# Second layer norm in another group order, and the last quarter of the output norm on ScalarE and GpSimd, in a decoder layer on one Trainium2 core

## The chip, the cores and the metric

The kernel runs on one core of a Trainium2 chip. The metric is device time in microseconds. The core's engines run their own instruction streams in order and wait for one another through semaphores: TensorE (PE, matrix multiply, transposes), VectorE (DVE), ScalarE (ACT), GpSimd (POOL) and SyncE (SP, which here only issues DMAs).

## The reference

One layer of a decoder trunk on 256 tokens of width 2048, in float32. Each of three sub-layers adds its output to the scaled residual and normalises:

```python
h = x
h = layer_norm(ALPHA * h + hybrid_mixer(h, ...), ln_g[0], ln_b[0])
h = layer_norm(ALPHA * h + memory_cross_attention(h, mem, ...), ln_g[1], ln_b[1])
h = layer_norm(ALPHA * h + conv_ffn(h, ...), ln_g[2], ln_b[2])      # the output

def layer_norm(x, g, b):
    mu = mean(x); var = mean((x - mu)**2)
    return (x - mu) * rsqrt(var + 1e-5) * g + b

def conv_ffn(h, w_up, conv_w, conv_b, w_down):
    u = causal_depthwise_conv3(h @ w_up) + conv_b     # 2 x 5632 columns
    a, g = split(u, 2)
    return (a * gelu(g)) @ w_down
```

## The kernel before, in words

Every large matrix product is done as three float32r products: both operands are split into a high part (a cast on ScalarE, L296) and a low part (a subtraction on VectorE, L297), and TensorE computes high x high, high x low and low x high (`mm3` at L311 to L313 with the weights stationary, `mm3x` at L319 to L321 with the activations stationary). Weights come in chunks of 128 x 1024 (512 KB) through SP's queue. There are four buffers of raw chunks, and three each of high and low parts.

The program is written in the order of the model and a scheduler sets the order on each engine, by priorities ("lanes": `first` before `split` before `mixer` before `proj`) and by a simulated time line. Where the code wants a certain order on one engine it adds one by hand with `after(ins, other)`, which makes `ins` come after `other` without a semaphore. That order is fixed at build time.

The residual `R` holds 2 x 128 tokens ("token 0" and "token 1" below are the two halves of 128 tokens) by 2048 columns.

**Output projections.** `to_residual` goes through five column groups (512, 512, 512, 256, 256 columns). The products of a group are added to `R` (L423) and its batch-norm statistics taken (L427). The last `late` groups are done for token 0 first and then for token 1, so that work on token 0 can lie beside token 1's matmuls: after token 0's last group, and after each group of token 1, `next(beside)` emits one more piece of that work. In the cross-attention's projection `late` is 4, so this loop holds the groups at columns 512, 1024, 1536 and 1792, of 24, 24, 12 and 12 matmuls for each token; in the FFN's down projection it is 1.

**Layer norm.** `statistics` aggregates the statistics of a token half (L1125), adds epsilon (L1126), and gets 1/sqrt from ScalarE as exp(-0.5 ln v) (L1127, L1128), with one Newton step in four small VectorE instructions (L1129 to L1132). `normalise` needs two VectorE instructions for each column group: subtract the mean and multiply by the gain (L1149), then multiply by 1/sqrt and add the bias (L1154). `layer_norm_of` then transposes 128-column tiles on TensorE (L1163), and `split_on_pe` makes the two parts in PSUM: cast on ScalarE (L1171), subtraction on TensorE by a product with a negated identity (L1172), cast again (L1174). These features are the right-hand side of the FFN's up projection, whose first three tiles (`to_rows_of`) go through features of columns 0 to 1023 first and 1024 to 2047 after.

In the second layer norm token 0 has four groups of 512 columns and token 1 has six (128, 128, 256, 512, 512, 512). With `NORM0 = 3` three groups of token 0 are emitted beside token 1's projection, and `NORM1 = (2,)` emits the fourth after token 1's third. `holds` puts the low part of the FFN's second and third weight chunk behind two of the normalise instructions, which `HOLD` picks from the list of them.

**The end.** `last_norm(0)` lies beside token 1's last column group, `last_norm(1)` follows it: four groups of 512 columns, each stored with a DMA, in turn from ScalarE's and SP's queue.

Of the kernel before, what the change touches and what calls it, by code (L numbers as in the profile page):

```python
# [8 lines left out]
F32 = mybir.dt.float32  # L9
# [6 lines left out]
D = 2048  # L16
# [19 lines left out]
CST_AT = 3  # L36
SKEW = 16
MOVING_AT = {512: 48, 256: 32}
NORM0, NORM1, HOLD = 3, (2,), 2
TABLE_PACE, SCAN_PACE = 0.8, 2.8  # L40
BUCKET_FROM = [16, 21, 27, 35, 46, 59, 77, 99, 128, 166, 216]

# [156 lines left out]
class Program:  # L199
    def __init__(self, tc, a, out, ctx):  # L200
        self.tc, self.nc, self.a, self.out, self.ctx = tc, tc.nc, a, out, ctx
        pool = lambda name, bufs, **kw: ctx.enter_context(tc.tile_pool(name=name, bufs=bufs, **kw))
        self.lanes = {"first": 0, "split": 100_000, "mixer": 200_000, "proj": 300_000,
                      "late": 400_000}
        self.cur_lane, self.turns = "mixer", False
        self.holds = []
        self.background, self.pace, self.credit = None, 0.0, 0.0
        self.last_hi = self.last_lo = self.last_mm = None
        self.mm_marks = [None, None, None]
        self.bv = Behind(self, self.nc.vector, lambda: self.last_lo)  # L210
        self.bs = Behind(self, self.nc.scalar, lambda: self.last_hi)
        self.bt = Behind(self, self.nc.tensor, lambda: self.mm_marks[-2])
        tc.cur_priority = self.lanes["mixer"]
        self.consts = pool("consts", 1)
        self.wraw = pool("wraw", 4)
        self.whi = pool("whi", 3)
        self.wlo = pool("wlo", 3)
        self.gap("a", 192)
        self.acts = pool("acts", 1)
        self.stat = pool("stat", 2)  # L220
        self.pj = pool("pj", 3, space=bass.MemoryType.PSUM)
        self.op = pool("op", 1, space=bass.MemoryType.PSUM)
        self.mx = pool("mx", 2, space=bass.MemoryType.PSUM)
        self.pq = pool("pq", 1, space=bass.MemoryType.PSUM)
        self.dram = pool("dram", 1, space=bass.MemoryType.DRAM)
# [89 lines left out]
    def mm3x(self, ps, hi, lo, ah, al, start, stop):  # L315

        mm = self.nc.tensor.matmul
        with self.lane("proj"):
            mm(ps, ah, hi, start=start, stop=False)  # L319
            mm(ps, ah, lo, start=False, stop=False)  # L320
            self.last_mm = mm(ps, al, hi, start=False, stop=stop)  # L321

# [37 lines left out]
    def to_residual(self, w, X, k0, k1, scaled=True, final=True, load=None, late=0, keep=(),  # L360
# [31 lines left out]
        for tok in range(2):  # L392
            left = [(k1 - k0) * n // 1024 for _, n in RES_COLS[early:]]
            ps = {}
            for i in order:
                g, c0, n, ks, src = chunks[i]
                if i not in held:
                    held[i] = self.weights(src, into=keep[i] if i in fixed else None, cols=n)
                new = g not in ps
                if new:  # L400
                    ps[g] = self.pj.tile([128, 512], F32, name="pj")
                left[g] -= 1
                self.chunk_cols(ps[g], held[i], X, tok, n, ks, new, left[g] == 0)
                if left[g] == 0:
                    self.add(ps[g][:, :n], tok, c0, n, scaled, final)
                    if beside is not None:
                        next(beside, None)
            if tok == 0:
                beside = between()
                next(beside, None)  # L410
                again = order[len(keep):-turning]
# [706 lines left out]
    def statistics(self, toks):  # L1118

        V, S, n = self.nc.vector, self.nc.scalar, len(toks)  # L1120
        with self.lane("first"):
            mv = self.stat.tile([128, 2, 2], F32, name="mv")
            v, y, t = (self.stat.tile([128, 2], F32, name=i)[:, :n] for i in ("vv", "yy", "ty"))
            for i, tok in enumerate(toks):
                V.bn_aggr(mv[:, i, :], self.st[:, tok])  # L1125
            V.tensor_scalar(v, mv[:, :n, 1], EPS, None, ALU.add)  # L1126
            S.activation(y, v, ACTF.Ln)  # L1127
            S.activation(y, y, ACTF.Exp, scale=-0.5)  # L1128
            V.tensor_mul(t, y, y)  # L1129
            V.tensor_mul(t, t, v)  # L1130
            V.tensor_scalar(t, t, -0.5, 1.5, ALU.mult, ALU.add)
            V.tensor_mul(y, y, t)  # L1132
        return [(mv[:, i, 0:1], y[:, i:i + 1]) for i in range(n)]

    def load_gb(self, i):
# [23 lines left out]
    def transposes(self, pairs):  # L1159

        last = None
        for dst, src in pairs:
            ins = self.nc.tensor.matmul(dst, src, self.ident, is_transpose=True,  # L1163
                                        start=last is None, stop=True, skip_group_check=True)
            if last is not None:
                self.after(ins, last)
            last = ins

    def split_on_pe(self, ps, h):

# [25 lines left out]
    def layer_norm_of(self, tok, H, edges):  # L1196
# [3 lines left out]
        for c0, c1 in self.normalise((tok,), norm, edges):  # L1200
            kk = min(4, (c1 - c0) // 128)
            for k in range(c0 // 128, c1 // 128, kk):
                ps = self.mx.tile([128, kk, 128], F32, name="mx")
                self.transposes([(ps[:, j, :], self.R[:, tok, (k + j) * 128:(k + j + 1) * 128])
                                 for j in range(kk)])
                self.split_features(ps, H, k, kk, slice(tok * 128, tok * 128 + 128))
            yield

# [70 lines left out]
    def ffn(self, H):  # L1279
# [2 lines left out]
        p = self.ctx.enter_context(self.tc.tile_pool(name="ffp", bufs=1))  # L1282
        w = self.ctx.enter_context(self.tc.tile_pool(name="ffw", bufs=2))
        cv = p.tile([128, NFF, 2, 4], F32, name="cv")
        nc.scalar.dma_start(cv, a["conv"].rearrange("p (i j c) -> p i j c", i=NFF, j=2))
        act = [self.acts.tile([128, KD, 2, 256], F32R, name="A", tag="A"),
               p.tile([128, NFF - KD, 2, 256], F32R, name="act")]
        act = Parts(*[t[:, i:i + 4] for t in act for i in range(0, t.shape[1], 4)])
# [24 lines left out]
            pass  # L1313

    def last_norm(self, tok):
        norm = self.statistics((tok,))
        for i, (c0, c1) in enumerate(self.normalise((tok,), norm, range(0, D + 1, 512))):
            (self.nc.sync if i % 2 else self.nc.scalar).dma_start(
                self.out[tok * 128:tok * 128 + 128, c0:c1], self.R[:, tok, c0:c1])
            yield  # L1320


# [19 lines left out]
```

## Time and profile before

| | |
|---|---|
| median of 3 runs | 1284.87 us (1282.33 to 1287.47) |
| the profiled execution | 1284.53 us |
| its span in the profile | 1282.4 us |
| TensorE busy | 1250.7 us (98%) |
| VectorE busy | 882.1 us (69%) |
| ScalarE busy | 659.7 us (51%) |
| GpSimd busy | 18.9 us (1%) |

The span is the time between the first and the last instruction or transfer that the profiler saw; start-up and completion lie around it. Times in rows count from the span's start. A row of the order of instructions has start, duration, engine, line, operation, output<-inputs, shape and count; in square brackets is the idle time of the engine before it and what ended it. A row of the table of stretches has the stretch, its length, then busy time and number of instructions of PE, PEld (weight load), DVE, ACT and POOL, the granted TensorE clock as a share of full speed, the DMA engines' share and GB/s. A busy TensorE is not a fast one: the number of matmuls in a stretch and the granted clock tell that.

### The profile page before, as it was taken

How to read it: one execution, taken by the hardware profiler on the slowest of the kernel's cores; microseconds unless marked ns; L12 is line 12 of the kernel's file. 1: busy time of each engine (PE TensorE's matmuls, PEld its weight loads, DVE VectorE, ACT ScalarE, POOL GpSimd, SP SyncE). 2: the span in 40 equal slices, each digit the busy share in tenths (PEclk: the TensorE clock that was granted, in tenths of full speed). 3: DMA queues.
4: the chain of work that ended last, by engine and by line, in shares of the span. 5: the costliest groups of instructions: out<-in, count | busy, mean ns of one | idle time of the engine just before them, and what ended most of it. 6: DMA issues, size and time to landing. Idle time of an engine off the chain costs nothing.

```text
span 1282.4 us, 23034 instructions
## 1 busy us (share of the span) xinstructions
PE 1250.7 (98%) x9222; PEld 1157.6 (90%) x9222; DVE 882.1 (69%) x1507; ACT 659.7 (51%) x1032; POOL 18.9 (1%) x34
## 2 busy tenths in 40 slices
PE   7999999899999999899999999999999999999996
PEld 7788889898789899699999999999999988888896
DVE  7899898777675666866666666666666654554557
ACT  6884436566563356355555555555555543334342
POOL 0200001000000000000000000000000000000000
PEclk9999999999999999999999999999999999999998
DMA  8663347743356554355555555655565755656573
GB/s 291 196 179 117 116 133 209 217 133 132 122 191 246 188 207 149 121 165 194 191 192 197 194 189 194 198 193 188 195 198 192 255 194 197 192 185 198 186 240 131
DMA packets 67350, 237.37 MB, mean 185 GB/s; under 512 B 7787, under 2 KB 8604, under 8 KB 66476
## 3 DMA queue, kind: packets, MB, share of 16 engines
q1 hardware_dynamic: 64720, 230.21, 54.4%
q0 software_dynamic: 1424, 4.33, 1.7%
q8 instruction: 72, 1.18, 0.4%
q10 hardware_dynamic: 1100, 1.38, 0.3%
q14 instruction: 34, 0.28, 0.1%
HBM read 231.82 MB, written 2.49 MB: 183 GB/s over the span
## 4 chain that ended last, share of the span: by engine, by line
PE 89%; DMA 4%; DVE 3%; ACT 3%; issue 1%; POOL 0%; SPq 0%; ACTq 0%; DVEq 0%
PE pj L311 17%; PE pj L313 17%; PE pj L312 17%; PE pj L319 10%; PE pj L320 10%; PE pj L321 10%; DMA raw<-in_win_u 2%; PE pa L1053 2%; DMA s5us<-Ec 1%; DMA raw<-in_win_c 1%; ACT hi L296 1%; PE pa L191 1%; DVE lo L297 1%; PE mx L882 1%; PE mx L1016 1%
## 5 line engine op out<-in xcount | busy, mean ns | idle before, releaser
L297 DVE TENSOR_TENSOR lo<-raw,hi 128x1024 fp32r<-128x1024 f32 (+2 forms) x403 | 488.5, 1212 | 338.1 <-ACT hi L296 336.6
L296 ACT CAST hi<-raw 128x1024 fp32r<-128x1024 f32 (+2 forms) x403 | 419.6, 1041 | 510.4 <-PE pj L312 279.1
L312 PE MATMUL pj<-mix,hi 128*128 128x256 f32 x1380 | 382.2, 277 | 0.0
L311 PE MATMUL pj<-mix,hi 128*128 128x256 f32 x1380 | 381.7, 277 | 0.0
L313 PE MATMUL pj<-mix,lo 128*128 128x256 f32 x1380 | 381.4, 277 | 0.0
L311 PEld LDWEIGHTS pj<-mix,hi 128*128 128x128 f32 x1380 | 259.6, 188 | 0.2
L312 PEld LDWEIGHTS pj<-mix,hi 128*128 128x128 f32 x1380 | 259.4, 188 | 0.1
L313 PEld LDWEIGHTS pj<-mix,lo 128*128 128x128 f32 x1380 | 259.4, 188 | 0.0
L311 PE MATMUL pj<-A,hi 128*128 128x256 f32 x496 | 140.7, 286 | 6.7 <-ACT hi L296 6.6
L313 PE MATMUL pj<-A,lo 128*128 128x256 f32 x496 | 138.7, 287 | 3.6 <-DVE lo L297 3.5
L312 PE MATMUL pj<-A,hi 128*128 128x256 f32 x496 | 139.2, 284 | 0.0
L311 PEld LDWEIGHTS pj<-A,hi 128*128 128x128 f32 x496 | 94.7, 192 | 9.5 <-ACT hi L296 7.5
L313 PEld LDWEIGHTS pj<-A,lo 128*128 128x128 f32 x496 | 93.4, 192 | 7.9 <-DVE lo L297 5.1
L320 PE MATMUL pj<-lo,act 128*128 128x512 f32 (+1 forms) x280 | 96.3, 345 | 0.0
L321 PE MATMUL pj<-hi,act 128*128 128x512 f32 (+1 forms) x280 | 96.3, 345 | 0.0
L312 PEld LDWEIGHTS pj<-A,hi 128*128 128x128 f32 x496 | 94.6, 192 | 1.6 <-issue 1.6
L320 PE MATMUL pj<-lo,A 128*128 128x512 f32 (+2 forms) x288 | 95.9, 334 | 0.0
L321 PE MATMUL pj<-hi,A 128*128 128x512 f32 (+2 forms) x288 | 95.4, 332 | 0.0
L319 PE MATMUL pj<-hi,A 128*128 128x512 f32 (+2 forms) x288 | 90.7, 333 | 0.0
L319 PE MATMUL pj<-hi,act 128*128 128x512 f32 (+1 forms) x280 | 89.3, 345 | 0.0
L320 PEld LDWEIGHTS pj<-lo,A 128*128 128x128 f32 x288 | 54.1, 188 | 6.5 <-issue 1.1
L321 PEld LDWEIGHTS pj<-hi,A 128*128 128x128 f32 x288 | 54.2, 188 | 5.0
(325 smaller groups left out, 1809.6 us busy)
## 6 DMA issues: line engine op xcount, KB each, us to landing
raw<-in_w_up SPq DMA_DIRECT2D x176, 512.0 KB, 3.4
raw<-in_w_down SPq DMA_DIRECT2D x92, 512.0 KB, 4.3
raw<-in_win_c SPq DMA_DIRECT2D x48, 512.0 KB, 4.3
raw<-in_w_out SPq DMA_DIRECT2D x32, 512.0 KB, 3.4
raw<-in_win_sv SPq DMA_DIRECT2D x8, 512.0 KB, 4.9
raw<-in_wk_m SPq DMA_DIRECT2D x8, 512.0 KB, 4.3
raw<-in_wv_m SPq DMA_DIRECT2D x8, 512.0 KB, 4.0
raw<-in_wq SPq DMA_DIRECT2D x8, 512.0 KB, 4.4
```

What stands on the lines that cost most here:

```text
L191: ins = getattr(self.engine, name)(*args, **kw)
L296: self.last_hi = nc.scalar.copy(hi[:, :n], raw[:, :n])
L297: self.last_lo = nc.vector.tensor_sub(lo[:, :n], raw[:, :n], hi[:, :n].bitcast(F32))
L311: mm(ps, hi, ah, start=start, stop=False)
L312: mm(ps, hi, al, start=False, stop=False)
L313: self.last_mm = mm(ps, lo, ah, start=False, stop=stop)
L319: mm(ps, ah, hi, start=start, stop=False)
L320: mm(ps, ah, lo, start=False, stop=False)
L321: self.last_mm = mm(ps, al, hi, start=False, stop=stop)
L882: mm(h_ps[:, 0:75].rearrange("p (g n) -> p g n", g=5), w1[:, i * 128:i * 128 + 128], kv[:, :, 2 * l:2 * l + 16 * NC_ - 15:16], start=l == ...
L1016: mm(zs, q[:, t, gl, qs], kh[:, 0:m], start=True, stop=False)
L1053: ins = mm(o[64 * r:64 * r + 64, gl, 128 * c:256], vv[:, c, v, :], pt[:, k0:k1], start=start[r] is None, stop=False, skip_group_check=True)
```

## The change

Five parts:

- The second layer norm emits two groups of token 0 beside token 1's projection in place of three (`NORM0`), and the other two after token 1's fourth and fifth group (`NORM1`). `HOLD` stays 2, but the list that it indexes has another order now: it picks token 1's third and fourth group, before token 1's third and token 0's fourth.
- TensorE's first matmul of token 1's third and fourth column group in that projection gets an order: after the last transpose of token 0's group 0 and group 1 (`behind`, `turned`).
- The Newton step has two instructions for each token half (scalar_tensor_tensor) in place of four; the first layer norm, which does both halves at once, has two for each half, so four in all as before.
- The convolution's constants are loaded from GpSimd's queue in place of ScalarE's.
- `last_norm(1)` does three groups of 512 columns on VectorE. The last 512 columns go through ScalarE (x / sqrt - mean / sqrt, with an offset from one small VectorE instruction) and two GpSimd instructions (times gain, plus bias), and are stored from SP's queue as before.

```diff
-NORM0, NORM1, HOLD = 3, (2,), 2
+NORM0, NORM1, HOLD = 2, (3, 4), 2
...
@@ mm3x
-            mm(ps, ah, hi, start=start, stop=False)
+            ins = mm(ps, ah, hi, start=start, stop=False)
+            if self.behind is not None:
+                self.after(ins, self.behind)
+                self.behind = None
@@ to_residual
                 if new:
                     ps[g] = self.pj.tile([128, 512], F32, name="pj")
+                    if beside is not None and 0 <= g - 2 < len(self.turned):
+                        self.behind = self.turned[g - 2]
...
             if tok == 0:
+                self.turned = []
                 beside = between()
@@ statistics
-            V.tensor_scalar(v, mv[:, :n, 1], EPS, None, ALU.add)
-            S.activation(y, v, ACTF.Ln)
+            V.tensor_scalar(v, mv[:, :n, 1], EPS, -0.5, ALU.add, ALU.mult)
+            S.activation(y, v, ACTF.Ln, scale=-2.0)
             S.activation(y, y, ACTF.Exp, scale=-0.5)
-            V.tensor_mul(t, y, y)
-            V.tensor_mul(t, t, v)
-            V.tensor_scalar(t, t, -0.5, 1.5, ALU.mult, ALU.add)
-            V.tensor_mul(y, y, t)
+            for i in range(n):
+                V.scalar_tensor_tensor(t[:, i:i + 1], y[:, i:i + 1], v[:, i:i + 1], y[:, i:i + 1],
+                                       ALU.mult, ALU.mult)
+                V.scalar_tensor_tensor(y[:, i:i + 1], t[:, i:i + 1], 1.5, y[:, i:i + 1],
+                                       ALU.add, ALU.mult)
@@ layer_norm_of (self.last_turn is the last transpose that transposes() issued)
                                  for j in range(kk)])
+                self.turned.append(self.last_turn)
@@ ffn
-        nc.scalar.dma_start(cv, a["conv"].rearrange("p (i j c) -> p i j c", i=NFF, j=2))
+        nc.gpsimd.dma_start(cv, a["conv"].rearrange("p (i j c) -> p i j c", i=NFF, j=2))
@@ last_norm
-        norm = self.statistics((tok,))
-        for i, (c0, c1) in enumerate(self.normalise((tok,), norm, range(0, D + 1, 512))):
-            (self.nc.sync if i % 2 else self.nc.scalar).dma_start(
-                self.out[tok * 128:tok * 128 + 128, c0:c1], self.R[:, tok, c0:c1])
+        nc, cut = self.nc, D - 512 * tok
+        norm = self.statistics((tok,))
+        rows, queues = slice(tok * 128, tok * 128 + 128), (nc.scalar, nc.sync)
+        if cut < D:
+            (mean, rstd), r = norm[0], self.R[:, tok, cut:]
+            off = self.stat.tile([128, 1], F32, name="off")
+            nc.vector.scalar_tensor_tensor(off, mean, -1.0, rstd, ALU.mult, ALU.mult)
+            nc.scalar.activation(r, r, ACTF.Identity, scale=rstd, bias=off)
+            nc.gpsimd.tensor_tensor(r, r, self.gb[:, 0, cut:], ALU.mult)
+            nc.gpsimd.tensor_tensor(r, r, self.gb[:, 1, cut:], ALU.add)
+        for i, (c0, c1) in enumerate(self.normalise((tok,), norm, range(0, cut + 1, 512))):
+            queues[i % 2].dma_start(self.out[rows, c0:c1], self.R[:, tok, c0:c1])
             yield
+        if cut < D:
+            queues[1].dma_start(self.out[rows, cut:], r)
```

More of the change, by code (lines that the diff above doesn't have):

```diff
@@ L318, in mm3x @@
         with self.lane("proj"):
-            mm(ps, ah, hi, start=start, stop=False)
+            ins = mm(ps, ah, hi, start=start, stop=False)
+            if self.behind is not None:
+                self.after(ins, self.behind)
+                self.behind = None
             mm(ps, ah, lo, start=False, stop=False)
@@ L1167, in transposes @@
             last = ins
+        self.last_turn = last
     def split_on_pe(self, ps, h):
```

## The prediction

> **What bounds the kernel now.** I read the page first, then the chain of waits by time, then the table of stretches around the three places that the diff touches (the second layer norm near 540 us, the FFN, the end), then the order of instructions on each engine there.
>
> The page:
> ```profile
> span 1282.4 us, 23034 instructions
> PE 1250.7 (98%) x9222; PEld 1157.6 (90%) x9222; DVE 882.1 (69%) x1507; ACT 659.7 (51%) x1032; POOL 18.9 (1%) x34
> ...
> PEclk9999999999999999999999999999999999999998
> ...
> PE 89%; DMA 4%; DVE 3%; ACT 3%; issue 1%; POOL 0%; SPq 0%; ACTq 0%; DVEq 0%
> ```
> TensorE is 98% busy and carries 89% of the chain that ended last; the clock row is at 9 everywhere but in the last slice. So the bound is the number of matmuls, and only stretches in which TensorE lacks work or runs slowly can be shortened. The FFN, which is more than half of the span, has nothing to give; the table of stretches:
> ```profile
> 600.00:700.00 100.00, 100.00 (x882) 100.00 (x881) 66.82 (x93) 52.48 (x75) 0.00 (x0) 1.00 0.58 194
> ```
> 882 matmuls in 100 us, 0.113 us each at full clock. What the diff can change lies in two stretches. The first is the second layer norm, same table:
> ```profile
> 537.00:539.00 2.00, 1.10 (x3) 0.53 (x4) 1.53 (x5) 1.89 (x6) 0.00 (x0) 1.00 0.32 90
> ...
> 543.00:545.00 2.00, 2.00 (x12) 2.00 (x12) 1.97 (x3) 0.76 (x3) 0.00 (x0) 0.50 0.00 0
> ```
> After the stretch's name stand its length and TensorE's busy part; the number after POOL is the granted clock. From 537 to 539 TensorE has little to do, from 543 to 545 it is busy at half clock. When the clock falls and rises, in narrower stretches:
> ```profile
> 62.50:63.00 0.50, 0.22 (x1) 0.22 (x2) 0.50 (x2) 0.50 (x2) 0.00 (x0) 0.73 0.00 0
> 66.00:66.50 0.50, 0.50 (x5) 0.50 (x5) 0.42 (x1) 0.50 (x2) 0.00 (x0) 0.86 0.00 0
> 540.50:541.00 0.50, 0.18 (x1) 0.00 (x0) 0.43 (x3) 0.29 (x1) 0.00 (x0) 0.60 0.00 0
> 547.00:547.50 0.50, 0.50 (x5) 0.50 (x4) 0.47 (x2) 0.09 (x1) 0.00 (x0) 0.58 0.00 0
> 1274.00:1276.00 2.00, 0.00 (x0) 0.00 (x0) 1.90 (x4) 0.00 (x0) 0.00 (x0) 0.62 0.07 27
> ```
> A mean of 0.73 in 62.50 to 63.00 puts a fall at 62.73; 0.86 puts the rise at 66.14; 0.60 puts a fall at 540.60, 0.58 the rise at 547.42, and 0.62 a fall at 1274.48. The distances are 3.41, 477.87 (140 x 3.413), 6.82 (2 x 3.41) and 733.88 (215 x 3.413): this execution decides on the clock every 3.413 us on a fixed grid, and 544.01 lies on it.
>
> The second stretch is the end: after the last matmul only VectorE works, and its order of instructions shows a row of normalise instructions, two for each 512 columns:
> ```profile
> 1273.46 0.15 DVE L1129 TENSOR_TENSOR ty<-yy 128x1 f32<-128x1 f32 x1
> 1273.64 0.16 DVE L1130 TENSOR_TENSOR ty<-ty,vv 128x1 f32<-128x1 f32 x1
> ...
> 1274.22 0.75 DVE L1154 SCALAR_TENSOR_TENSOR R<-R,yy,gb 128x512 f32<-128x512 f32 x1
> ...
> 1277.12 0.75 DVE L1154 SCALAR_TENSOR_TENSOR R<-R,yy,gb 128x512 f32<-128x512 f32 x1
> ...
> 1278.57 0.75 DVE L1154 SCALAR_TENSOR_TENSOR R<-R,yy,gb 128x512 f32<-128x512 f32 x1
> ```
>
> **The change, part by part.**
>
> *Second layer norm, token 0.* Two of its four groups, not three, now come during token 1's output projection; the other two come after token 1's fourth and fifth group. And TensorE is told to do the transposes of groups 0 and 1 ahead of the first matmul of token 1's third and fourth column group. From the chain, the third column group starts at 532.89:
> ```profile
> 532.89 0.12 PE pj L319
> ```
> Orders on VectorE, ScalarE and TensorE around it:
> ```profile
> 531.91 0.75 DVE L1154 SCALAR_TENSOR_TENSOR R<-R,yy,gb 128x512 f32<-128x512 f32 x1
> ...
> 533.84 0.74 DVE L1154 SCALAR_TENSOR_TENSOR R<-R,yy,gb 128x512 f32<-128x512 f32 x1
> ...
> 536.42 0.40 DVE L423 SCALAR_TENSOR_TENSOR R<-R,pj 128x256 f32<-128x256 f32 x1
> 536.75 0.74 DVE L1154 SCALAR_TENSOR_TENSOR R<-R,yy,gb 128x512 f32<-128x512 f32 x1
> 537.41 0.42 DVE L427 BATCH_NORM_STATS2 st<-R 128x6 f32<-128x256 f32 x1
> ...
> 538.19 0.15 DVE L1126 TENSOR_SCALAR vv<-mv 128x1 f32<-128x1 f32 x1
> ...
> 540.26 0.16 DVE L1129 TENSOR_TENSOR ty<-yy 128x1 f32<-128x1 f32 x1 [1.67 <-ACT yy L1128]
> ...
> 541.04 0.35 DVE L1154 SCALAR_TENSOR_TENSOR R<-R,yy,gb 128x128 f32<-128x128 f32 x1
> ```
> ```profile
> 538.32 1.14 ACT L1174 CAST mix<-mx 128x384 fp32r<-128x384 f32 x2
> 539.35 0.21 ACT L1127 ACTIVATE yy<-vv 128x1 f32<-128x1 f32 x1
> 539.54 0.59 ACT L1171 CAST mix<-mx 128x512 fp32r<-128x512 f32 x1
> 540.02 0.21 ACT L1128 ACTIVATE yy<-yy 128x1 f32<-128x1 f32 x1
> ```
> ```profile
> 535.09 0.60 PE L1163 MATMUL mx<-cst,R 128*128 128x128 f32 x4
> ...
> 535.88 0.28 PE L321 MATMUL pj<-hi,ox 128*128 128x256 f32 x1
> ...
> 540.18 0.50 PE L1172 MATMUL mx<-mix,nident 128*128 128x512 f32 x1 [0.67 <-ACT mix L1171]
> ...
> 542.62 0.95 PE L311 MATMUL pj<-mixk,hi 128*128 128x256 f32 x3
> ```
> Token 0's first group is normalised at 531.91 + 0.75 = 532.66, just ahead of 532.89, its second at 533.84 + 0.74 = 534.58. The third column group is 12 matmuls of 0.113 us (1.4 us), so the fourth starts near 532.89 + 0.60 of transposes + 1.4 = 534.9: neither order should hold TensorE. But transposes and the split matmuls that now come before the last matmul (535.88) delay it by the second set of transposes and by the split of group 0; a set of four took at most 0.60 and a split 0.50, and they overlap their neighbours: I take 0.8 (bounds 0.3 and 1.1). Last matmul: 536.7.
>
> From there token 1's chain. Before, its last addition at 536.42 was followed by a normalise of token 0's third group (536.75), and the statistics came at 537.41, 0.99 after. That normalise goes; the addition took 0.40; gain 0.59. The variance is ready at 538.19, but Ln starts at 539.35, behind the splits (1.14 in the row at 538.32), and Exp behind another cast (539.54): VectorE waited 1.67 for it. Third-group casts are gone here; a weight cast and the second group's split stay. Bounds 0 and 1.67, taken 1.3, nearer the upper since the queue ahead is what goes. The Newton step needs two small instructions in place of four: from 540.26 to 541.04 is 0.78 for four, gain 0.39. Sum: 541.04 + 0.8 - 0.59 - 1.3 - 0.39 = 539.56, 1.5 us earlier, and the FFN's first matmul moves from 542.62 to 541.1.
>
> *The clock.* Before, 542.62 to 547.42 is 4.8 us at half clock, 2.4 us of work lost. At 540.60 the clock falls again, since the sparse stretch from 537.0 to 541.1 still covers the interval before it. The next decision is at 544.01: before, that interval was dense for 1.4 of 3.41 us and the clock stayed low; now for 2.9, and the interval of 62.73 to 66.14, dense but for its start, was enough for a rise. So half clock from 541.1 to 544.01, 1.45 lost, a gain of 0.95. Bounds: no rise until 547.42 loses 3.15 (0.75 worse than before); no fall at all gains 2.4. I take 0.95.
>
> The Trainium skill, "TensorE: Matmul & The Clock Gate", Part 1, has the same window of 3413 ns, which agrees with the 3.41 here, and calls it free-running, so that the phase differs from run to run; by it, an estimate, 4.1 us of sparse work can miss a full window in some executions. One trace cannot show that.
>
> *What moves behind.* Token 0's third group: its transposes and split lay in the empty stretch and now lie among FFN matmuls; at most 0.60 + 0.50, taken 0.7, lost. Its normalise adds 1.5 us to VectorE. Cover: the features of columns 1024 on are needed only after 8 x 3 x 3 = 72 matmuls (8.1 us at full rate, plus 1.45 for the clock, from 541.1: not before 550.6). VectorE from 539.56: some 2.0 for the three short groups (0.35 for one instruction of 128 columns, 0.74 for 512), two low parts of 1.21 each, and three groups of 1.5 give 548.5, and about 2 us of transposes, casts and split follow: just in time. If that cover fails, TensorE waits some tenths. The held low parts:
> ```profile
> L297 DVE TENSOR_TENSOR lo<-raw,hi 128x1024 fp32r<-128x1024 f32 (+2 forms) x403 | 488.5, 1212 | 338.1 <-ACT hi L296 336.6
> ```
> The second weight chunk's low part stays behind the same group, the third's moves from token 0's last group to token 1's fourth: nothing, covered by the same 72 matmuls; a slip would cost at most one such 1.21.
>
> Layer norm sum: 1.5 + 0.95 - 0.7 = 1.75 us gained.
>
> *First layer norm.* Two tokens at once: four small instructions become four. Nothing.
>
> *The convolution's constants* go from ScalarE's queue to GpSimd's:
> ```profile
> L571 POOL MEMSET Ec<- 128x1536 f32 x1 | 1.4, 1378 | 0.3 <-POOLq L1331 0.3
> L868 POOL DMA_DIRECT2D kv<-in_cpos x2 | 1.1, 564 | 6.6 <-DMA g_dr<-oh 5.7 <-DVE pb L887 0.9
> ```
> ```profile
> 561.38 0.56 ACT L1296 ACTIVATE cy<-pj,cv 128x256 f32<-128x256 f32 x1
> ```
> ScalarE loses that issue, whose gain is part of the 1.3 above. GpSimd issues in 0.56 with nothing behind it, and the first use is at 561.38; token 1's chain doesn't touch it. Nothing.
>
> *The end.* Token 0's last norm keeps its columns; its shorter Newton step lies under dense matmuls. Token 1: the new small instructions stand where those at 1273.46 and 1273.64 do, the offset for ScalarE follows one step of 0.19 later, and the first large instruction starts at 1274.03 in place of 1274.22. VectorE keeps three groups: its last ends at 1277.12 + 0.75 - 0.19 = 1277.68, not 1278.57 + 0.75 = 1279.32: 1.64 us gained. Beside it ScalarE: 0.56 for 256 columns with both pointers (row at 561.38), so for 512 at most 1.12 and no less than the 0.59 of its cast of 512 at 539.54; taken 0.8, between, done near 1274.85. Then two GpSimd instructions, which no run shows. GpSimd's write of 1536 columns took 1.378, so 0.46 for 512; that is the lower bound; two reads and a write one after another, 1.38, the upper. I take the upper, the operation with three streams being nearest to it: done at 1277.6, just hidden; beyond 1.42 each they set the end. The last two stores then start almost together instead of 1.45 apart:
> ```profile
> out<-R SPq DMA_DIRECT2D x4, 256.0 KB, 2.0
> ```
> 2.0 to landing each: between nothing and 2.0 more; they share the transfer engines only in part, taken 0.3. SP's queue has nothing behind that store. Tail: 1.3 gained.
>
> Sum: 1.75 + 1.3 = 3.05. The profiled execution took 1284.53 (span 1282.4 and 2.1 around it), 0.34 under the median of 1284.87. So 1281.5 against its own time and **1281.8** against the median.
>
> **Rivals.**
> 1. *The clock doesn't fall.* If the grid lies otherwise, no interval is sparse enough. For it: the sparse stretch shrinks from 6.5 us (535.88 + 0.28 to 542.62) to 4.1. Against: the fall at 62.73 needed far less. Gains 1.5 + 2.4 - 0.7 + 1.3 = 4.5: 1280.4.
> 2. *The clock stays low until 547.42.* The layer norm then gives 1.5 - 0.75 - 0.7 = 0.05: the reordering doesn't do what it says, and only the tail counts: 1283.5. For it: matmuls at half clock between transposes may count as sparse; against: the rise at 66.14.
> 3. *VectorE and GpSimd shut each other out at the end.* Then VectorE's 3.65 us and GpSimd's two instructions add up: 1274.03 + 3.65 + 0.92 to 2.76 is 1278.6 to 1280.4, against 1279.32; in the middle 0.2 lost, with the stores 0.5. 1.75 - 0.5: 1283.6. Against: the trace has no GpSimd arithmetic at all. The Trainium skill, "SBUF — State Buffer", Who interferes with whom, states just this lock for a VectorE instruction with two SBUF inputs beside a GpSimd one that reads; no run here shows it.
> 4. *Slower: TensorE held at the third column group.* If VectorE's order puts token 0's two groups behind token 1's additions, TensorE waits with the column groups queued behind the transposes. Were group 0 ready only at 537.49 (the row at 536.75) and group 1 one pair of 1.5 later, the last matmul is near 541.5, 4.8 us after 536.7: 4.8 - 3.05 = 1.75 slower, 1286.6. It decides from a hold of 3.05 us. Against: 532.66 and 534.58 are in time.
>
> **How the numbers follow.** Forecast 0.30, rivals 0.20, 0.20, 0.22, 0.08. The range must take in the first rival with its upper bounds (1.64 in the tail, a delay of 0.3: about 1279), the second and third, and most of the fourth: 1278.5 to 1286.5; the forecast's own is 1280.5 to 1283. A difference of 0.5% is 6.4 us, about what runs from 1282.33 to 1287.47 can tell. No case reaches it in either sum; the first with something unseen gives 0.09 for faster, the fourth 0.04 for slower, 0.87 for the same.
>
> **What would show it.** The last projection matmul near 536.7, both token 0 transposes before it, Ln close behind the variance, token 1's first large normalise near 539.6; clock rise near 544 or no fall; two GpSimd rows of at most 1.4 us that end before VectorE's last; VectorE's last 1.6 us earlier relative to the last matmul. Wrong if TensorE shows a wait for VectorE ahead of a transpose near 533, GpSimd rows of 2 us, or VectorE idle between its last normalises.

## The result, and the profile after

The changed kernel is slower: 1302.24 us (median of 4, 1301.14 to 1305.99) against 1283.61 for the kernel before beside it, ratio 1.0148 [1.012, 1.0175]. The profiled execution took 1305.99 us, its span 1304.2; it is the slowest of the four. The prediction said 1281.8, with a range that ended at 1286.5, and is wrong by 20 us, 17 of them in matmuls that the diff doesn't touch. One of the eleven runs of e5_old_tail below took 2082.85 us, at a granted clock of 0.556, and is left out of its median.

The page after, the rows that answer to those of before:
```profile
span 1304.2 us, 23043 instructions
PE 1268.3 (97%) x9222; PEld 1172.6 (90%) x9222; DVE 881.5 (68%) x1498; ACT 659.7 (51%) x1033; POOL 22.6 (2%) x37
...
PEclk9999999899999999899999999999999999999998
...
PE 90%; DMA 4%; ACT 3%; DVE 2%; issue 1%; POOL 0%; SPq 0%; ACTq 0%; DVEq 0%
```
TensorE has the same 9222 matmuls, yet is busy 1268.3 us in place of 1250.7. The chain still runs through it (90%). Of the 21.8 us by which the span grew, 17.6 are busy time of the same matmuls, so most of the loss isn't waiting. Where, the table of stretches says in its first 100 us of steady FFN (number of matmuls behind TensorE's busy part, granted clock after GpSimd's column):
```profile
600.00:700.00 100.00, 100.00 (x858) 100.00 (x858) 64.58 (x90) 50.84 (x71) 0.00 (x0) 1.00 0.58 187
```
858 matmuls in place of 882, at a clock of 1.00, with TensorE busy for all of it: no wait, and no lower clock. Its order of instructions shows which (start, duration, engine, line):
```profile
701.21 0.28 PE L314 MATMUL pj<-mix,lo 128*128 128x256 f32 x1
701.33 0.28 PE L312 MATMUL pj<-mix,hi 128*128 128x256 f32 x1
701.45 0.28 PE L313 MATMUL pj<-mix,hi 128*128 128x256 f32 x1
...
703.09 0.28 PE L312 MATMUL pj<-mix,hi 128*128 128x256 f32 x1
703.20 0.28 PE L313 MATMUL pj<-mix,hi 128*128 128x256 f32 x1
703.32 0.28 PE L314 MATMUL pj<-mix,lo 128*128 128x256 f32 x1
...
704.79 0.28 PE L312 MATMUL pj<-mixk,hi 128*128 128x256 f32 x1
```
From 701.21 on, matmuls on the feature tiles mix0 and mix1 start 0.12 us apart; from 703.09 on, in the same weights' rhythm, those on mix2 and mix3 start 0.113 apart (rows leave a tile's number out; the loop over the feature blocks gives it, back from the next mixk at 704.79). Before, both were 0.113 apart. Mean spacings from the starts in the two traces, before and after: 113.4 and 120.0 ns on mix0 and mix1, 113.3 in both on mix2 and mix3 (600 to 1000 us, without the first two or three matmuls after a change of tile, which are up to 122 ns apart in both); 116.1 and 117.8 on mixk; in the down projection's matmuls of 512 columns 226.7 and 233.3 on act, 226.8 and 227.0 on the A tile.

Of the tiles that the FFN's matmuls read, the slower ones are just those that the change moved. The new tile `off` (4 bytes a partition, two buffers of 32 bytes) lies in the statistics' pool, and everything that is allocated on that side of SBUF after it lies 64 bytes higher: mix1 at byte 96544 in place of 96480, mix0, mixk and act likewise; hi, lo, A, mix2 and mix3 stay.

### The profile page after: what moved, and what is told of

The parts are those of the page before. It is cut to its first block, busy times and chain, and to the rows that moved or that the text cites. A ratio compares the mean times of both kernels' runs of the same rounds, so it can differ in the third digit from the quotient of the medians.

```text
span 1304.2 us, 23043 instructions
## 1 busy us (share of the span) xinstructions
PE 1268.3 (97%) x9222; PEld 1172.6 (90%) x9222; DVE 881.5 (68%) x1498; ACT 659.7 (51%) x1033; POOL 22.6 (2%) x37
## 4 chain that ended last, share of the span: by engine, by line
PE 90%; DMA 4%; ACT 3%; DVE 2%; issue 1%; POOL 0%; SPq 0%; ACTq 0%; DVEq 0%
PE pj L312 17%; PE pj L314 17%; PE pj L313 17%; PE pj L320 10%; PE pj L324 10%; PE pj L325 10%; PE pa L1060 2%; DMA raw<-in_win_c 1%; ACT hi L297 1%; DMA s5us<-Ec 1%; PE pa L191 1%; DMA raw<-in_win_u 1%; PE mx L889 1%; PE mx L1023 1%; PE mx L1024 1%
## 5 line engine op out<-in xcount | busy, mean ns | idle before, releaser
L313 PE MATMUL pj<-mix,hi 128*128 128x256 f32 x1380 | 386.7, 281 | 0.0
L312 PE MATMUL pj<-mix,hi 128*128 128x256 f32 x1380 | 386.3, 281 | 0.0
L314 PE MATMUL pj<-mix,lo 128*128 128x256 f32 x1380 | 385.7, 280 | 0.0
L325 PE MATMUL pj<-hi,act 128*128 128x512 f32 (+1 forms) x280 | 97.7, 350 | 0.0
L320 PE MATMUL pj<-hi,act 128*128 128x512 f32 (+1 forms) x280 | 90.7, 350 | 0.0
L325 PEld LDWEIGHTS pj<-hi,act 128*128 128x128 f32 x280 | 52.6, 188 | 7.6
```

The source lines that it names most:

```text
L312: mm(ps, hi, ah, start=start, stop=False)
L313: mm(ps, hi, al, start=False, stop=False)
L314: self.last_mm = mm(ps, lo, ah, start=False, stop=stop)
L320: ins = mm(ps, ah, hi, start=start, stop=False)
```

## Experiments

### Placement or order

Placement (P): the 64 bytes make the matmuls slower, and only the remainder of the address in some period counts. Order (Q): the new order of instructions does it.

`e1_same_place`: the changed kernel, with `off` in a buffer of an old tile, so that nothing moves.
```
-off = self.stat.tile([128, 1], F32, name="off")
+off = self.stat.tile([128, 2], F32, name="ty")[:, :1]
```


> The changed kernel, except that the new one-column tile `off` takes a buffer that the statistics pool has already (ty), so that no tile behind that pool moves. Theory P (placement: the 64 bytes that `off` adds move mix0, mix1, mixk and act, and matmuls that read them get slower): spacing of the FFN matmuls on mix0 and mix1 back from 120.0 to 113.4 ns, 882 matmuls per 100 us, and 1281 to 1285 us. Rival Q (the new order of the second layer norm changes the FFN's order of instructions for good): 858 matmuls per 100 us and about 1302 us as in the changed kernel.


`e2_before_64`, `e3_before_128`, `e4_before_256`: the kernel before with so many unused bytes behind the statistics' pool.
```
 self.stat = pool("stat", 2)
+self.gap("s", 64)      # 128, 256
```


> The kernel before, with 64 unused bytes a partition behind the statistics pool and nothing else. P: mix0, mix1, mixk and act stand where they stand in the changed kernel, so 120 ns on mix0 and mix1, 113.4 on mix2 and mix3, 858 matmuls per 100 us and 1300 to 1304 us. Q: nothing changes, 1283.6 us.

> The kernel before, with 128 unused bytes there. P with a period of 128 bytes or less (P128): as before, 113.4 ns and 1283.6 us. P with a period of 256 (P256): the features then stand at 96 modulo 256, neither the 224 of before nor the 32 of the changed kernel, which is also the remainder of the weight parts; if only an equal remainder costs, about 113.4 ns and 1284 us, and if 224 is special, slower by up to 18 us. Q: 1283.6 us.

> The kernel before, with 256 unused bytes there. P256: the same remainders as before, 113.4 ns and 1283.6 us. P with a longer period: 116 to 120 ns on mix0 and mix1, 1290 to 1302 us. Q: 1283.6 us.


Measured: e1 1286.37 us, ratio to before 1.0014 [1.0004, 1.0024]; e2 1301.31, 1.0132 [1.0118, 1.0146]; e3 1306.04, 1.0173 [1.0159, 1.0186]; e4 1284.04, 1.0000 [0.9991, 1.0009]. The same stretch in e1, in e2 and in e3:
```profile
600.00:700.00 100.00, 100.00 (x881) 100.00 (x881) 65.65 (x92) 53.18 (x74) 0.00 (x0) 1.00 0.58 192
```
```profile
600.00:700.00 100.00, 100.00 (x858) 100.00 (x858) 64.71 (x90) 51.34 (x72) 0.00 (x0) 1.00 0.57 190
```
```profile
600.00:700.00 100.00, 100.00 (x852) 100.00 (x851) 64.01 (x89) 50.39 (x70) 0.00 (x0) 1.00 0.56 187
```
e1 has all of the change and 881 matmuls; e2 has nothing of it but the 64 bytes, and 858. Q falls, P holds, and e4 with e3 gives the period, 256 bytes. One row of e3 didn't fit: mix2 and mix3 had not moved, and slowed to 117.8 ns as well; so e3 lost 22 us, where at most 18 had been expected.

### Which distance counts

Four more placements, to tell a tile's own address from its distance to the weights' tile (hi and lo, at remainder 32 of 256 before).
```
 p1_all_64     +self.gap("w", 64)   ahead of the raw weights' pool: all tiles of that side move
 p2_right_128  +128 unused bytes ahead of mix2 and mix3 alone
 p3_before_192 +self.gap("s", 192)  as e2
 p4_before_32  +self.gap("s", 32)   as e2
```


> The kernel before with an empty 64 bytes ahead of the raw weights' pool, so that every tile on the left side moves by 64: the weights' hi and lo from remainder 32 (of 256) to 96, mix0, mix1 and act from 224 to 32; mix2 and mix3 stay at 224. Own address: if a feature tile's own remainder sets the spacing, mix0 and mix1 take 120.0 ns as in the changed kernel and mix2 and mix3 113.3, about 1300 us. Distance: if it is the distance between the weights' tile and the feature tile, mix0 and mix1 (192 as before) take 113.3, and it is mix2 and mix3 (now 128) that may change; were they unchanged too, 1284 us.

> The kernel before with an empty 128 bytes ahead of mix2 and mix3 on the right side: these move from remainder 224 to 96, all tiles of the left side (mix0, mix1, mixk, act, hi, lo) stay. With 128 bytes on the left, mix0 and mix1 took 117.7 ns and so did mix2 and mix3, though these had not moved. Each tile for itself: mix2 and mix3 117.7, mix0 and mix1 113.3: 88 tiles of the up-projection x 21 matmuls x 4.4 ns = 8 us slower than before, 1292. Carried over: if a pace that is once begun goes on into the next tile, both take the same, 117.7 (1284 + 48 x 88 x 4.4 ns = 1303) or 113.3 (1284).

> The kernel before with 192 empty bytes behind the statistics' pool: mix0, mix1 and act at remainder 160, mixk at 96, mix2 and mix3 unmoved at 224. Placement with a period of 256: a fourth point between 117.7 ns (+128) and 113.3 (+256); a steady slope would give 115 ns and 1291 us, bounds 113.3 and 120.0, 1284 and 1302. Were it not the remainder but any shift that is not 256, 117 ns or more and 1300 us.

> The kernel before with 32 empty bytes behind the statistics' pool: mix0, mix1 and act at remainder 0, mixk at 192. If only the remainder of 64 counts (all remainders so far were 32 of 64), 113.3 ns and 1284 us; if the position in 256 counts, half of the step to +64, some 116 to 117 ns and 1292 us, or already 120.0 and 1301.


One run of each, against 1281.48 for before: 1300.34, 1293.88, 1294.64, 1305.56. The slopes that were expected of the last two (115 ns, 116 to 117) were wrong: 118.5 and 118.3. Distance is the feature tile's address minus that of the weights, modulo 256. In the up-projection the weights are the stationary operand and the features move past them; in the down projection act is stationary and the weights move, from 192 bytes into their tile on (`MOVING_AT`). Then the mean spacing in the trace, counted as above:
```
                 mix0, mix1           mix2, mix3           down projection
                 distance  ns         distance  ns         act - weights  ns
before, +256     192       113.4      192       113.3      0              226.7
+64, changed       0       120.0      192       113.3      64             233.3
+128              64       117.8      192       117.8      128            232.4
+192             128       118.5      192       113.3      192            228.9
+32              224       118.3      192       117.8      32             233.3
all +64          192       115.7      128       118.7      0              226.7
right -128       192       113.5       64       117.8      0              226.7
```
Own address falls: in "all +64", mix0, mix1 and act lie at the remainder that gave 120.0 and 233.3 ns, but as far from the weights as before, and take 115.7 and 226.7. Distance holds where it can be compared: 128 gives 118.5 and 118.7 with two different addresses, 64 gives 117.8 in both runs. mixk, three matmuls at the head of each tile, fits: it lies at distance 0 before (116.1 ns), at 64 in "+64" (117.8), at 128 in "+128" (118.3), and in "+192" at 192, where it takes 113.3. (By the allocated addresses its remainder is 224 in p3 and 64 in p4; the 96 and 192 expected above are wrong.) In the up-projection 192 is the only fast distance of those seen. It is not always fast: in "all +64" the 70 tiles of the stretch alternate, 35 with 113 to 113.5 ns and 35 with 117.5 to 118, and in "+128" and "+32" mix2 and mix3 hold 117.8 though nothing of theirs moved. That looks like two paces, of which the half of a tile keeps the one that it began with; what chooses it stays open. A slow pace isn't always carried on: in "right -128" mix0 and mix1 follow slow matmuls and are back at 113 ns after four. Why 192 is fast no run shows.

Another engine's writes into the weights' tiles could also be what the features' address meets. The cross-attention's projection speaks against that. In its pass for token 1 the features' tile (ox) is stationary and kept weights move, at the same seven distances as act, and neither is written to meanwhile. Its matmuls of 512 columns are 226.6, 233.3, 232.5, 229.0, 233.4, 226.6 and 226.6 ns apart, in the order of the rows: the last column again. What is left is the distance between TensorE's own two operands.

The Trainium skill, "SBUF — State Buffer", Who interferes with whom, lists two read ports for TensorE, one for the moving operand and one for the weights' load, as independent. Read so, the distance would not matter; the 113.3 to 120.0 ns measured here say that it does.

What 64 bytes cost, from the starts in the traces of before and e2: an up-projection tile of 48 matmuls takes 5.607 us in place of 5.460, in 88 tiles 12.9 us; 504 matmuls of 512 columns on act x 6.6 ns = 3.3, and 336 of 256 columns x 3.0 ns (118.7 in place of 115.7) = 1.0. That is 17.2, against 1301.31 - 1284.13 = 17.2 measured.

### The prediction's own terms, with the tiles in place

With `off` out of the way the change is still 0.14% slower, 1.8 us, where 3.05 of gain had been summed. Its parts:
```
 e5_old_tail     e1 with last_norm as before
 e6_old_ln2      e1 with  NORM0, NORM1 = 3, (2,)  and without the order after self.turned
 e7_tail_memset  e1 with  nc.gpsimd.memset(r, 0.0)  twice for the two nc.gpsimd.tensor_tensor
 e9_newton_only  before with the short Newton step and cv on GpSimd's queue
```


> The changed kernel with its last norm as before (so the small tile off is gone too, and all tiles lie as before): the new order of the second layer norm, the short Newton step and the constants' queue alone. Against the changed kernel with off placed apart (1286.4): if VectorE and GpSimd hold each other up at the end (their rows there were 1.63 and 1.75 us instead of 0.75, 1.51 and 1.59), 0.6 to 1 us faster; if the new tail gains the 1.3 of the prediction, 1.3 slower. Against before: the layer norm's 3.6 us up to 566 us given back to 0.4, so 0 to 0.5 us faster, 1284; had nothing been given back, 3 us faster.

> The changed kernel with off placed apart and the old order of the second layer norm (three groups of token 0 beside token 1, one behind its third, no order between transposes and column groups): new tail, short Newton step and constants' queue alone. Lock at the end: 0.3 to 1 us slower than before, 1285; the prediction's tail: 1.3 faster, 1282.8. No stall of TensorE of 1.8 us near 566 us if that belongs to the new order.

> The changed kernel with off placed apart; in the last norm GpSimd's multiplication and addition for the last quarter are replaced by two fills with zero (gain and bias of token 1's last 512 columns are left out). If VectorE is held up by GpSimd's reads (a lock), its rows of 1.63 and 1.75 us near the end return to 0.75 and its last ends 1.6 us earlier relative to the last matmul, as the prediction's tail had it. If any GpSimd work beside it slows it, they stay above 1.2.

> The kernel before with two parts of the change alone: the short Newton step and the constants' load on GpSimd's queue; order of the second layer norm and last norm as before. The run with these two and the new tail was at 1.0001, and its tail lay 0.8 us longer in the trace. Sum of parts: 0.8 us less than that, 0.5 to 1 us faster than before (1283.2), its interval just touching 1; the last addition to the end 0.25 shorter than before. If the Newton step's gain is lost to the clock's grid, no difference to before.


Measured against before: e9 1282.94 us, 0.9999 [0.999, 1.0008]; e6 1283.45, 1.0001 [0.9992, 1.0009]; e5 1285.56, 1.0010 [1.0001, 1.002]; e7 one run, 1287.29. e9 had been expected 0.5 to 1 us faster. So the Newton step and the queue are worth nothing that can be measured, the tail no gain, and the new order of the second layer norm seems to cost 0.1% (e5's interval and e9's overlap) in place of the 1.75 us that it should gain.

*The tail.* VectorE and then GpSimd at the end of e1, each in order of start:
```profile
1273.04 0.42 DVE L430 SCALAR_TENSOR_TENSOR R<-R,pj 128x256 f32<-128x256 f32 x1 [1.77 <-PE pj L325]
...
1276.19 0.74 DVE L1158 SCALAR_TENSOR_TENSOR R<-R,mv,gb 128x512 f32<-128x512 f32 x1
1276.97 1.63 DVE L1163 SCALAR_TENSOR_TENSOR R<-R,yy,gb 128x512 f32<-128x512 f32 x1
1278.52 1.75 DVE L1158 SCALAR_TENSOR_TENSOR R<-R,mv,gb 128x512 f32<-128x512 f32 x1
1280.30 0.75 DVE L1163 SCALAR_TENSOR_TENSOR R<-R,yy,gb 128x512 f32<-128x512 f32 x1
```
```profile
1276.55 1.51 POOL L1336 TENSOR_TENSOR R<-R,gb 128x512 f32<-128x512 f32 x1 [736.64 <-ACT R L1335]
1278.13 1.59 POOL L1337 TENSOR_TENSOR R<-R,gb 128x512 f32<-128x512 f32 x1
```
The same on VectorE and GpSimd in e7, where GpSimd only writes (gain and bias of token 1's last 512 columns are left out):
```profile
1275.85 0.42 DVE L430 SCALAR_TENSOR_TENSOR R<-R,pj 128x256 f32<-128x256 f32 x1 [1.77 <-PE pj L325]
...
1279.78 0.75 DVE L1163 SCALAR_TENSOR_TENSOR R<-R,yy,gb 128x512 f32<-128x512 f32 x1
1280.45 0.75 DVE L1158 SCALAR_TENSOR_TENSOR R<-R,mv,gb 128x512 f32<-128x512 f32 x1
1281.23 0.75 DVE L1163 SCALAR_TENSOR_TENSOR R<-R,yy,gb 128x512 f32<-128x512 f32 x1
```
```profile
1279.33 0.53 POOL L1336 MEMSET R<- 128x512 f32 x1 [739.29 <-ACT R L1335]
1279.91 0.53 POOL L1337 MEMSET R<- 128x512 f32 x1
```
Beside GpSimd's two instructions, VectorE's take 1.63 and 1.75 us in place of 0.75, and GpSimd's 1.51 and 1.59. When GpSimd reads nothing, VectorE is back at 0.75, so it is GpSimd's reads that hold it up (the lock). From the start of the last addition to the end of the span: before 1282.4 - 1271.49 = 10.91, e1 1284.7 - 1273.04 = 11.66, e7 1285.5 - 1275.85 = 9.65. The tail lost 0.75 where a gain of 1.3 was forecast. With a GpSimd that only writes it gains 1.26; how long the two reading instructions take with VectorE out of their way no run shows. From VectorE's last end to the end of the span it is 3.08 us before, 3.65 in e1 and 3.52 in e7, so the stores, taken at 0.3, cost 0.57 and 0.44. The Trainium skill's section named above states this lock for a VectorE instruction with two SBUF inputs beside a GpSimd one that reads, and exempts a GpSimd one that only writes: both agree here, at 1.63 and 1.75 against 0.75.

*The second layer norm.* The gain of its front came out near the forecast. VectorE's order in e1, where a stage before it, with the same instructions in both, had put everything 2.1 us later than in the trace of before:
```profile
538.78 0.42 DVE L430 SCALAR_TENSOR_TENSOR R<-R,pj 128x256 f32<-128x256 f32 x1 [1.01 <-PE pj L325]
...
540.02 0.15 DVE L1134 TENSOR_SCALAR vv<-mv 128x1 f32<-128x1 f32 x1
...
541.15 0.22 DVE L1138 SCALAR_TENSOR_TENSOR ty<-yy,vv 128x1 f32<-128x1 f32 x1 [0.72 <-ACT yy L1136]
541.40 0.16 DVE L1140 SCALAR_TENSOR_TENSOR yy<-ty,yy 128x1 f32<-128x1 f32 x1
541.60 0.35 DVE L1163 SCALAR_TENSOR_TENSOR R<-R,yy,gb 128x128 f32<-128x128 f32 x1
```
From token 1's last addition to its first large normalise 2.82 us, against 541.04 - 536.42 = 4.62 before: 1.80 gained. TensorE's last projection matmul comes 0.48 later than before, the addition behind it 0.26, which leaves 1.54. But behind it TensorE stands still, in the FFN (e1, stretches of 1 us, then the waits of 545 to 570 us, then VectorE's and TensorE's orders):
```profile
565.00:566.00 1.00, 0.63 (x6) 0.43 (x4) 1.00 (x3) 1.00 (x3) 0.00 (x0) 1.00 0.00 0
566.00:567.00 1.00, 0.00 (x0) 0.00 (x0) 1.00 (x2) 1.00 (x2) 0.00 (x0) 1.00 0.65 168
567.00:568.00 1.00, 0.56 (x5) 0.59 (x6) 1.00 (x3) 0.38 (x1) 0.00 (x0) 1.00 0.85 340
```
```profile
PE pj L312 <- ACT cy L1307: 1.8, 1, 1.8
```
```profile
564.15 1.23 DVE L298 TENSOR_TENSOR lo<-raw,hi 128x1024 fp32r<-128x1024 f32 x1 [5.76 <-ACT hi L297]
565.29 0.47 DVE L1308 SCALAR_TENSOR_TENSOR cy<-pj,cv,cy 128x255 f32<-128x255 f32 x1
565.68 1.21 DVE L298 TENSOR_TENSOR lo<-raw,hi 128x1024 fp32r<-128x1024 f32 x1
566.82 0.47 DVE L1310 SCALAR_TENSOR_TENSOR cy<-pj,cv,cy 128x254 f32<-128x254 f32 x1
```
```profile
565.35 0.28 PE L314 MATMUL pj<-mix,lo 128*128 128x256 f32 x1
567.44 0.36 PE L312 MATMUL pj<-mixk,hi 128*128 128x256 f32 x1 [1.81 <-ACT cy L1307]
```
The fourth up-projection tile needs the first tile's PSUM buffer. VectorE is the last to read it, in the instruction at 566.82, behind two low parts of weights (564.15 and 565.68) that wait until the first tiles' weights are used up. The page of waits names ScalarE's cy, which ended long before. In e1's order on TensorE the last features' split comes 98 FFN matmuls in (65 before), so the first three tiles are worked on side by side and end 1.4 us apart in place of 2.7, and nothing covers the release. In e7 the clock falls a second time behind the same stall:
```profile
567.00:568.00 1.00, 0.00 (x0) 0.00 (x0) 1.00 (x2) 1.00 (x3) 0.00 (x0) 1.00 0.59 147
568.00:569.00 1.00, 0.48 (x4) 0.51 (x5) 1.00 (x3) 0.46 (x1) 0.00 (x0) 0.98 0.88 332
...
572.00:573.00 1.00, 1.00 (x9) 1.00 (x9) 0.43 (x1) 0.46 (x2) 0.00 (x0) 0.81 0.91 270
```
A fall at 568.96 and a rise near 572.4 lose another 1.7 us. What lets it fall there and not in e1 no run shows.

The traces of e1 and e5 show no second fall. At the stage's start the clock is low for one interval in them, but for two in the trace of before. In e4, which has the instructions of before at the same distances, it is low for one, so e4 is what the stage is to be compared with:
```profile
541.00:542.00 1.00, 0.84 (x6) 0.87 (x6) 0.96 (x4) 0.54 (x3) 0.00 (x0) 0.75 0.00 0
...
544.00:545.00 1.00, 1.00 (x7) 1.00 (x6) 1.00 (x2) 0.00 (x0) 0.00 (x0) 0.55 0.82 258
```
Times from token 0's first matmul at columns 1536 on, from the starts in the traces (each group has 12 matmuls for each token): the first FFN matmul starts after 17.92 us in e4, after 16.36 in e1 and 16.35 in e5, so 1.6 is gained. The last matmul of the seventh up-projection tile starts after 62.00 in e4, 62.69 in e1 and 62.60 in e5: 0.6 to 0.7 lost. With the old order and the short Newton step it is 61.99 (e6) and 61.68 (e9), the clock low for one interval again. So the new order gives back over 2 us, 1.8 of them in the stall. The trace of before, at 63.24, makes e1 and e5 look 0.5 to 0.6 faster, by its clock alone. A second fall in a part of the runs may add to the loss (e1's three slowest of 11, 1287.51 to 1288.22 us, have a mean clock of 0.989 to 0.990 as e7 has, its others 0.992 to 0.994), but only e7's trace shows one. e5, expected to be level with before or up to 0.5 us faster, was 1.3 slower.

`e8_turns_early`, `e10_turns_later`: e5, with an order on TensorE that brings the last transposes and splits forward (half, i and k count the weights' half, the up-projection tile and the feature block of the matmul that comes behind them).
```
+if len(ts) == 3 and (half, i, k) == (0, 2, 4):  self.behind = self.last_turn    # e10: (0, 2, 6)
+if len(ts) == 3 and (half, i, k) == (1, 0, 8):  self.behind = self.last_split   # e10: (1, 0, 10)
...                  (mm3 passes `behind` on to its first matmul, as mm3x does)
```


> The changed kernel with the last norm as before, and two orders more on TensorE: the last transposes of the second layer norm come ahead of the 13th matmul of the third up-projection tile's first half (61 FFN matmuls in, not 74), and the last matmul of the features' split ahead of the second half of the first tile (84 in, not 98). Theory (the gain is given back because the last features are turned and split late, so the first three tiles end nearly together and the fourth waits for a PSUM buffer that VectorE frees behind two low parts): the first tile ends 1 to 2.5 us earlier, the stall of 1.8 us shrinks below 0.6, 1 to 2 us faster than the run with only the last norm as before, 1.5 to 2.5 faster than the kernel before. Rival (VectorE's work of the second layer norm is the limit whatever TensorE's order): the wait only moves ahead of the transposes, within 0.4 us of it.

> As the run with the last features turned and split early, but ahead of the 19th matmul of the third tile's first half and of the third feature tile of the second half: transposes 67 FFN matmuls in (61 there, 74 in the changed kernel), splits 80 and 90 in. There TensorE still stood still for 0.39 us at 553, waiting for VectorE ahead of the transposes, and for 0.40 near 565. If the first hold came of turning too early it goes (0.4 us), and the second grows to no more than 0.9: within 0.5 us of that run, 1 us faster than the kernel with its last norm as before. If the stall of 1.8 us comes back, as slow as that one, 1285.6.


e8: 1283.79 us, 0.9994 [0.9986, 1.0003]; e10: 1283.47, 1.0002 [0.9992, 1.0012]. The waits of TensorE from 545 to 570 us, e8, then e10:
```profile
PE pj L312 <- DVE cy L1317: 0.4, 1, 0.4
```
```profile
PE pj L312 <- ACT cy L1314: 1.7, 1, 1.7
```
In e8 the stall shrinks from 1.8 to 0.4 us, and the kernel is 1.8 us faster than e5 (1285.56), as expected, though the two intervals just overlap. The 1.5 to 2.5 us by which it was to beat the kernel before didn't come: its trace, with the clock low for two intervals, takes 63.77 us to the seventh tile's end, where before, low for two as well, takes 63.24. In e10, whose last split comes only 8 matmuls ahead of e5's (e8's 14), the stall is back. For that case 1285.6 was expected, and 1283.47 came, not to be told from e5's or e8's by the intervals. So the traces show the stall, and the runs its price only roughly. None of e6, e8, e9 and e10 is to be told from the kernel before: no version here beats it.

## Why the prediction was wrong

1. *The bound.* Read rightly: TensorE's matmuls. But "the FFN has nothing to give" was taken as if it also had nothing to lose. The step that failed is in the tail: "the offset for ScalarE follows one step of 0.19 later" priced the new tile's instruction and not its memory. No term, bound or rival had it; it cost 17 us, more than five times the sum. The kernel before hints at it: its `self.gap` calls and `MOVING_AT` do nothing but set addresses.
2. *Token 1's chain*: 1.54 us measured in e1, 1.5 forecast, out of two misses: VectorE still waits 0.72 us for Exp (1.3 of 1.67 was to go, 0.95 went; all of the front 1.80 for 2.28), and the last addition moved by 0.26 in place of 0.8. That the two misses cancel is luck.
3. *The clock*: 0.95 was credited to the change; as far as the traces show, it belongs to the execution that was profiled. In e1 the clock is low for one interval, in the changed kernel's trace for two:
```profile
543.00:544.00 1.00, 1.00 (x8) 0.92 (x8) 0.97 (x2) 0.53 (x2) 0.00 (x0) 0.83 0.00 0
544.00:547.00 3.00, 3.00 (x16) 3.00 (x15) 2.96 (x4) 0.92 (x3) 0.00 (x0) 0.50 0.40 135
547.00:548.00 1.00, 1.00 (x11) 1.00 (x10) 0.96 (x3) 0.29 (x1) 0.00 (x0) 0.96 0.30 119
```
```profile
543.00:544.00 1.00, 0.32 (x1) 0.18 (x1) 0.93 (x4) 0.00 (x0) 0.00 (x0) 0.58 0.05 17
544.00:549.00 5.00, 4.64 (x22) 4.52 (x22) 4.93 (x8) 1.71 (x6) 0.00 (x0) 0.50 0.31 104
549.00:550.00 1.00, 1.00 (x7) 1.00 (x7) 0.96 (x2) 0.00 (x0) 0.00 (x0) 0.51 0.29 41
```
The falls and rises are at 543.66 and 547.08 (3.42 us) and at 543.16 and 549.98 (6.82). The page "TensorE: Matmul & The Clock Gate", Part 1, of the Trainium skill calls the window free-running; the two agree with that. The second rival is what the changed kernel's own trace shows. But the kernel before has both states as well: low for 6.82 us in its own trace, for 3.4 in e4's (541.50 to 544.90), where the stage is 1.24 us shorter without any change of its instructions.
4. *What moves behind*: "just in time", with "some tenths" if the cover fails. It failed: 1.8 us, and 1.7 more in e7, where the clock falls behind it. The cover was counted in matmuls up to the first use; what ended last was a PSUM release behind them.
5. *The tail*: wrong in sign, +0.75 for -1.3. The third rival was this one, given 0.22 and a loss of 0.2 with 0.3 for the stores. GpSimd's instruction was bounded by 1.38 and took 1.51 to 1.59, in the lock. The stores cost 0.57 for the 0.3 taken; that they share the transfer engines only in part no run shows.
6. *TensorE held at the third column group*: didn't happen. In the changed kernel (TensorE's order) the transposes start at 536.41 and 538.34, with no wait ahead of them:
```profile
536.41 0.60 PE L1172 MATMUL mx<-cst,R 128*128 128x128 f32 x4
...
538.34 0.62 PE L1172 MATMUL mx<-cst,R 128*128 128x128 f32 x4
```
7. *Newton step, constants*: forecast some 0.8 (0.39 at each of two places) and nothing; e9 shows 1280.8 - 1270.20 = 10.60 from the last addition to the end, 0.31 less than before, and no time that can be measured.

With the tiles in place the sum misses by 1.8 + 3.05 = 4.9 us. The terms that failed come to 4.8: 2.05 by the tail, 1.8 by the stall, 0.95 by the clock. They are read from single traces, the 4.9 from medians, so the close agreement is not a proof.

## What to carry to other kernels

A tile has an address as well as a size: before a diff is priced by its instructions, compare where the matmuls' operands lie before and after, modulo 256 bytes, and put a small new tile where nothing lies behind it, or into a buffer that exists. A count of matmuls in a steady stretch (882 or 858 in 100 us) shows at a glance whether such a shift has happened. Work given to GpSimd beside VectorE instructions with two SBUF inputs is not parallel if it reads; and time gained ahead of a long ordered queue is kept only if the next buffer's release moves too. Before a stage of two traces is compared, see that the clock is low for the same time in both.

## What was not expected of the hardware

The spacing of dense matmuls depends on where the weights' and the moving tile lie to each other in SBUF: 113.3 ns at the best of the five distances seen, 117.8 to 120.0 at the others, with a period of 256 bytes, and two paces at the same distance. In the 512-column matmuls it is 226.7 at 0, 228.9 at 192, and 232.4 to 233.3 at 32, 64 and 128. A stall of 1.8 us in a dense stretch can be followed by a clock of 0.50 for 3.4 us (e7), or not (e1, e5).
